# The low parts of the weights in the RWKV stage: computed by GpSimd, not by VectorE

## The chip, the cores and the metric

The kernel runs on one core of a Trainium2 chip. A core has TensorE (PE, matrix multiplication; its loading of weights is shown apart, as PEld), VectorE (DVE), ScalarE (ACT), GpSimd (POOL), the sync engine SP, whose queue issues most of the DMAs, and 16 DMA engines. Each engine works through its own instructions in order and waits on semaphores for the others. The metric is the time of one execution on the device, in microseconds, and less is better.

## The reference

It computes one step of a decoder layer with four head groups side by side, for a prompt of 1024 tokens and for 8 samples of one token each. Cut to what matters here:

```python
h = rmsnorm(x)
p = h @ w_in                       # one projection, split into columns of the four groups
out_a = diff_attn(...)             # A: differential attention
# B: RWKV-7, a recurrent state per head
s = s * w_t + (s @ a_t) * b_t + v_t * k_t
y = s @ r_t
out_b = group_norm(y) ... * silu(rg)
out_m = ssd_scan(...)              # C: Mamba-2
out_x = cross_attention(...)       # X: 256 memory tokens
x = x + concat(out_a, out_b, out_m, out_x) @ w_out
y = rmsnorm(x)
```

All of it is in float32. The results are the two outputs and the new caches and states.

## The kernel before, in words

The projection with `w_in` and the one with `w_out` are the bulk of the work on PE. To keep the accuracy of float32, each operand is split into a high part and a low part, and each product is made of three matmuls: high by high, high weight by low activation, low weight by high activation. In the profile they are `acc<-hh,whi`, `acc<-hl,whi` and `acc<-hh,wlo` (line 564). The activations are split once and stay in SBUF (`hh`, `hl`), in three groups of 344 token columns.

The weights come in pieces: 512 rows by 128 columns, held as a tile of 128 x 512. A piece is loaded by a DMA of SP's queue (`raw`, line 524), ACT makes the high part by a copy with rounding (`whi`, line 540), and DVE makes the low part, `raw` minus `whi` (`wlo`, line 541). `piece` asks for the next piece's split when it hands out the current one, so that PE has a whole piece of matmuls, 36 in the usual case, in which the next one is prepared. `raw`, `whi` and `wlo` have two buffers each.

The rest of the layer runs in stages beside the projections. A `Driver` takes turns: generators ("lanes") issue the instructions of the mixers, and between them it issues matmuls of the projection, a batch at a time. Each lane yields an estimate of how long it wants to let pass, and `K.now` counts the time of the matmuls issued. The framework then puts the instructions of each engine in order by priority and by its own estimate of when each is ready; the order on each engine is fixed before the program runs. An instruction that moves to another engine thus also moves others.

The change is in the stage of group B (RWKV), opened as `pool("bp")` in `step`. Its lanes are `elements` (for each of 16 units of 64 tokens: decays, normalised keys `kk`, the products `ar` and `bk`), `products` (Gram matrices `p_gram`, the inverse of a triangular block by doubling, the state `S` and the outputs), `norm` (the group norm of each unit's `y`) and `lane_b` (the 8 samples). The doubling in `products` is a chain between PE and DVE: PE adds to `p_t` (line 186 by the helper `mm`), DVE transposes a part of it (`xc`, line 970) and multiplies it with a mask (`lt`, line 972), ACT copies the other part (`rt`, line 978), and PE adds the next product. Four such rounds stand in each unit, after a first one whose `lt` is made in lines 950 to 952.

POOL has little to do in the stage: it fills and copies small tiles (`pe` line 885, `pc` line 888, `rt` line 954, `evx` line 706), raises to the power -1/2 in `powm` (line 216, for `rn` in `elements` and `gst` in `norm`), and issues the DMAs of the samples' states (lines 1162 and 1183). DVE waits for the powers: `rx` (line 799) for `rn`, and `y` (line 1087) for `gst`.

Of the kernel before, what the change touches and what calls it, by code (L numbers as in the profile page):

```python
# [11 lines left out]
F32 = mybir.dt.float32  # L12
# [3 lines left out]
ALU = mybir.AluOpType  # L16
# [116 lines left out]
class Kern:  # L133
# [363 lines left out]
    def plan_weights(self):  # L497

        p, w = [], self.I["w_in"]
        for name, j in ORDER[:FIRST] + ORDER:  # L500
            p += [(w, OFF[name] + j * 128, 8 if name == "mdt" else 128, kp) for kp in KO_IN]
        for i in range(2):
            for cb in range(16):
                p += [(self.I["w_out"], cb * 128, 128, kp) for kp in KO_OUT]
        self.plan, self.at, self.loaded, self.raw, self.split = p, 0, 0, {}, {}
        self.ahead, self.large, self.more = 2, None, None

    def load_pieces(self, to):
        while self.loaded < min(to, len(self.plan)):
# [17 lines left out]
    def split_piece(self, i):  # L527
        if i >= len(self.plan):
            return
        nc, m = self.nc, self.plan[i][2]  # L530
        raw = self.raw.pop(i)
        hi = self.wp.tile([128, KP, 128], F32R, name="whi", tag="whi")
        if m == 8:
            nc.vector.memset(raw[:, :, 8:32], 0.0)
            nc.scalar.copy(hi[:, :, :32], raw[:, :, :32])
            nc.vector.tensor_tensor(hi[:, :, 32:40], raw[:, :, :8], hi[:, :, :8].bitcast(F32), op=ALU.subtract)
            self.split[i] = hi, None
            return
        lo = self.wp.tile([128, KP, 128], F32R, name="wlo", tag="wlo")
        nc.scalar.copy(hi, raw)  # L540
        nc.vector.tensor_tensor(lo, raw, hi.bitcast(F32), op=ALU.subtract)  # L541
        self.split[i] = hi, lo

    def piece(self, src, c0, kp):
# [546 lines left out]
def shift_out(K, P):  # L1091

    nc = K.nc
    e = P.tile([9, 1664], F32, name="she", tag="she")
    for a in range(0, 13, 4):
        n = min(4, 13 - a)
        yield 0.5
        p = K.ps("p_sh", 1)
        for j in range(n):
            K.tp(p[:9, j * 128:j * 128 + 128], K.rawB[:, a + j, :], K.id)  # L1100
        nc.scalar.copy(e[:, a * 128:(a + n) * 128], p[:9, :n * 128])
    nc.sync.dma_start(out=K.O["shift_prompt"], in_=e[0:1, :])
    nc.sync.dma_start(out=K.O["shift_sample"], in_=e[1:9, :])
# [870 lines left out]
def projections(K):  # L1974

    W = K.I["w_in"]
    allg = list(range(NG))
    gates = {"rg": (4, "b"), "dg": (0, "a"), "xg": (12, "x")}
    evac = dict(dk=lambda j: EvPlain(K.sA[4 + j]), dv=lambda j: EvPlain(K.sA[8 + j]), dq=lambda j: EvPlain(K.sA[j], 0.125),
                mxbc=EvConv, mz=lambda j: EvSilu(K.sg[j]), xq=lambda j: EvPlain(K.sX[j], 128 ** -0.5), rs=EvShift)  # L1980

    def ready(*names):
        for n in names:
            while not K.have(n):
                yield False


    yield from ready("macc", *(f"h{g}" for g in FIRST_G))
    for name, j in ORDER[:FIRST]:
        yield from K.block(W, OFF[name] + j * 128, FIRST_G, evac[name](j), KO_IN)  # L1990
        K.turn += 1
    yield from ready("h1", "h2")
    for i, (name, j) in enumerate(ORDER):
        if name == "mdt":
            yield from K.block_dt()
        else:
            if name in gates:
                o, m = gates[name]
                yield from ready(m, "s" + m)
                ev = EvGate(o + j)  # L2000
            else:
                ev = evac[name](j)
            yield from K.block(W, OFF[name] + j * 128, [g for g in allg if i >= FIRST or g not in FIRST_G], ev, KO_IN)
        K.mark(f"{name}{j}")


def lane_x(K):

    pool = lambda n: K.tc.tile_pool(name=n, bufs=1)
    yield from K.wait("xq3", 9.00)  # L2010
    with pool("xap") as P:
        a, b = mixer_x(K, P, (0, 1)), mixer_x(K, P, (2, 3))
        for _ in range(200):
            for g in (a, b):
                r = next(g, "end")
                if r != "end":
                    yield r * 0.7
    K.mark("x")


def lane_b(K):

    pool = lambda n: K.tc.tile_pool(name=n, bufs=1, side="right")
    yield from K.wait(f"rs{RS[-1]}", 2.0)
    with pool("so") as P:
        yield from shift_out(K, P)
    yield 14.00
    with pool("sbp") as P:
        yield from samples_b(K, P)
    K.mark("sb")  # L2030


def lane_dt(K, P, P2):
    K.dt = yield from mamba_dt(K, P, P2)


def lane_m(K):
    yield from K.wait("mz3", 0.00)
    with K.tc.tile_pool(name="mmp", bufs=1, side="right") as P:
        yield from mixer_m(K, P, K.dt)  # L2040
    K.mark("m")


def lane_sa(K):

    pool = lambda n: K.tc.tile_pool(name=n, bufs=1, side="right")
    with pool("sap") as P:
        yield from samples_a(K, P)
    K.mark("sa")
    with pool("sxp") as P:  # L2050
        yield from samples_x(K, P)
    K.mark("sx")


def lane_s(K):
    yield 10.0
    with K.tc.tile_pool(name="mmr", bufs=1) as P:
        yield from samples_m(K, P, K.dt)
    K.mark("sm")


def step(ctx, tc, I, O):
    K, nc = Kern(ctx, tc, I, O), tc.nc
    pool = lambda n: tc.tile_pool(name=n, bufs=1)
    K.plan_weights()
    D = Driver(K, projections(K))
    with pool("xp") as P:
        mem = K.memory(P)
        next(mem)
        D.run([K.load_h(P), mem], batch=8)  # L2070
    with pool("ap") as P:
        D.run([mixer_a(K, P)], batch=8)
    with pool("cst") as P:
        K.cst[1] = P.tile([128, CST[1].shape[1]], F32, name="cst1", tag="cst1")
        nc.sync.dma_start(out=K.cst[1], in_=I["cst1"])
        D.run([lane_x(K), lane_sa(K)], batch=8)
    with pool("bp") as P:
        D.run(Rwkv(K, P).lanes() + [lane_b(K)], batch=4, slack=SLACK)
    with pool("mdt") as P:
        with pool("mdp") as P2:  # L2080
            D.run([lane_dt(K, P, P2)])
        D.run([lane_m(K), lane_s(K)], batch=4)
    output(K, D)
# [53 lines left out]
```

## Time and profile before

| | |
|---|---|
| time, median of 3 runs | 2157.11 us (2155.78 to 2159.48) |
| the profiled execution | 2158.15 us, its span 2156.4 us |
| PE busy in the span | 2091.5 us (97%) |
| PEld busy | 1983.5 us (92%) |
| DVE busy | 1146.5 us (53%) |
| ACT busy | 840.2 us (39%) |
| POOL busy | 201.2 us (9%) |
| mean granted TensorE clock | 0.991 of full speed |

The span runs from the first instruction to the last. PE is busy nearly all the time, so an engine beside it matters where PE stands still for it; how much that is in a stage is the difference between the stage's length and PE's busy time in it. A busy PE is not a PE at its peak, as matmuls overlap in the records: the mean of one accumulating matmul is 325 ns, while they follow each other at about half of that.

### The profile page before, as it was taken

To read this page: it belongs to the slowest core of one execution; us is meant where nothing else is said; L and a number is where in the kernel's file an instruction comes from. 1 tells how busy PE (TensorE), PEld (TensorE's weight loads), DVE (VectorE), ACT (ScalarE), POOL (GpSimd) and SP (SyncE) were. 2 spreads that over 40 slices of the span, in tenths; PEclk is the share of its full clock that TensorE was granted. 3 is DMA by queue.
4 is the path that set the end of the run, shared out by engine and by line. 5 is a ranking of instruction groups with operands and counts; after the bars stand their busy time and mean duration, and the time that the engine had idled before them with its cause. 6 is when DMAs were issued, how large, how long until landed. Compare 5 with 4: busy or idle time off the path is not lost.

```text
span 2156.4 us, 41670 instructions
## 1 busy us (share of the span) xinstructions
PE 2091.5 (97%) x16260; PEld 1983.5 (92%) x16260; DVE 1146.5 (53%) x2795; ACT 840.2 (39%) x2231; POOL 201.2 (9%) x286
## 2 busy tenths in 40 slices
PE   8999999999999999999999999998999999999997
PEld 6799999999999989988888888898999999999997
DVE  6814353543753152168977776656865254333554
ACT  7724353443233112145454454432112144333544
POOL 2100000000621320111110001001100000000000
PEclk9999999999999999999999999999999999999999
DMA  8653435242953562423322222226554763222891
GB/s 263 190 135 87 129 89 139 78 117 68 272 149 93 153 197 71 130 66 77 75 61 61 53 61 59 60 75 168 159 147 118 204 212 107 74 68 74 243 247 53
DMA packets 336925, 263.12 MB, mean 122 GB/s; under 512 B 62204, under 2 KB 310986, under 8 KB 336032
## 3 DMA queue, kind: packets, MB, share of 16 engines
q1 hardware_dynamic: 323744, 218.64, 36.2%
q0 software_dynamic: 12320, 40.28, 6.4%
q8 instruction: 128, 2.10, 0.4%
q10 hardware_dynamic: 664, 1.54, 0.2%
q14 instruction: 69, 0.57, 0.1%
HBM read 205.65 MB, written 54.80 MB: 121 GB/s over the span
## 4 chain that ended last, share of the span: by engine, by line
PE 80%; DVE 7%; DMA 3%; ACT 3%; issue 3%; POOL 1%; SPq 0%; ACTq 0%; DVEq 0%; POOLq 0%
PE acc L564 64%; PE p_s L1506 2%; PE p_t L186 2%; PE p_o L186 2%; DVE evc L715 1%; DVE wlo L541 1%; PE p_wt L190 1%; PE p_out L190 1%; PE acc L582 1%; DMA raw<-in_w_in 1%; PE p_xo L186 1%; POOL gst L216 1%; PE p_yd L186 1%; PE p_w L186 0%; PE p_xs L186 0%
## 5 line engine op out<-in xcount | busy, mean ns | idle before, releaser
L564 PE MATMUL acc<-hh,whi 128*128 128x344 f32 x3312 | 1074.7, 325 | 11.2 <-ACT haB L682 4.6
L564 PE MATMUL acc<-hl,whi 128*128 128x344 f32 x3312 | 1079.2, 326 | 0.1
L564 PE MATMUL acc<-hh,wlo 128*128 128x344 f32 x3312 | 1077.5, 325 | 0.8 <-DVE wlo L541 0.2
L564 PEld LDWEIGHTS acc<-hh,whi 128*128 128x128 f32 x3312 | 625.6, 189 | 17.3 <-ACT haB L682 4.8
L564 PEld LDWEIGHTS acc<-hl,whi 128*128 128x128 f32 x3312 | 626.9, 189 | 6.5 <-issue 1.4
L564 PEld LDWEIGHTS acc<-hh,wlo 128*128 128x128 f32 x3312 | 623.8, 188 | 7.7 <-DVE wlo L541 2.6
L541 DVE TENSOR_TENSOR wlo<-raw,whi 128x512 fp32r<-128x512 f32 x300 | 207.2, 691 | 476.5 <-ACT whi L540 468.0
L540 ACT CAST whi<-raw 128x512 fp32r<-128x512 f32 x300 | 185.5, 618 | 459.3 <-PE acc L564 392.5
L186 PEld LDWEIGHTS p_t<-rt,lt 64*64 64x64 f32 x1280 | 44.8, 135 | 33.1 <-issue 13.2
L1830 ACT ACTIVATE p_out<-xo 128x128 f32<-128x128 f32 (+1 forms) x144 | 39.8, 277 | 79.5 <-DVE xo L1829 75.1
L186 PE MATMUL p_t<-rt,lt 64*64 64x64 f32 (+1 forms) x1280 | 54.6, 224 | 15.2 <-DVE lt L972 8.4
L1509 DVE CUSTOM_DVE_ANT_0 ae<-p_s,al 128x512 f32<-128x512 f32 (+3 forms) x96 | 49.6, 554 | 34.6 <-PE p_s L1506 34.6
L1829 DVE TENSOR_TENSOR xo<-xo,p_out 128x128 f32<-128x128 f32 (+1 forms) x144 | 39.4, 280 | 26.6 <-PE p_out L190 26.4
L1516 ACT ACTIVATE ae<-ae,am 128x128 f32<-128x128 f32 (+7 forms) x64 | 49.2, 772 | 11.0 <-DVE am L1513 10.9
L978 ACT COPY rt<-p_t 128x256 f32<-128x256 f32 x64 | 22.0, 343 | 76.5 <-DVE xc L970 72.4
L216 POOL TENSOR_TENSOR osr<-osr,mhalf 128x1 f32<-128x1 f32 (+1 forms) x9 | 6.3, 721 | 472.8 <-DMA xo<-in_x_prompt 349.0
L541 DVE TENSOR_TENSOR wlo<-oraw,whi 128x512 fp32r<-128x512 f32 x48 | 33.2, 692 | 31.7 <-ACT whi L540 31.4
L216 POOL TENSOR_TENSOR ass<-ass,mhalf 128x8 f32<-128x8 f32 x4 | 6.6, 1641 | 423.3 <-DVE ass L1557 423.3
L1506 PE MATMUL p_s<-akm,aqt 128*128 128x512 f32 (+3 forms) x192 | 45.1, 359 | 0.0
L1617 POOL DMA_INDIRECT savp<-in_cache_diff_v,sapt x32 | 34.1, 1064 | 109.1 <-PE p_sao L186 100.5
L540 ACT CAST whi<-oraw 128x512 fp32r<-128x512 f32 x48 | 29.6, 617 | 32.4 <-PE acc L564 31.1
L1832 DVE TENSOR_TENSOR xo<-xo,fgc 128x128 f32<-128x128 f32 (+1 forms) x96 | 27.0, 288 | 28.7 <-ACT p_out L1830 26.2
(467 smaller groups left out, 2597.2 us busy)
## 6 DMA issues: line engine op xcount, KB each, us to landing
raw<-in_w_in SPq DMA_DIRECT2D x220, 256.0 KB
raw<-in_w_out SPq DMA_DIRECT2D x80, 256.0 KB
oraw<-in_w_out SPq DMA_DIRECT2D x12, 1024.0 KB
evm<-sm SPq DMA_DIRECT2D x48, 172.0 KB
sB<-evs SPq DMA_DIRECT2D x39, 172.0 KB
sA<-evp SPq DMA_DIRECT2D x36, 172.0 KB
evo<-so SPq DMA_DIRECT2D x36, 172.0 KB
sm<-evo SPq DMA_DIRECT2D x36, 172.0 KB
```

What stands on the lines that cost most here:

```text
L186: self.nc.tensor.matmul(out, lhsT=lhsT, rhs=rhs, start=start, stop=stop, **k)
L190: self.nc.tensor.transpose(out, in_, ident)
L216: self.nc.gpsimd.tensor_tensor(out, x, self.mhalf[:P, :n], op=ALU.pow)
L540: nc.scalar.copy(hi, raw)
L541: nc.vector.tensor_tensor(lo, raw, hi.bitcast(F32), op=ALU.subtract)
L564: nc.tensor.matmul(acc[g][:, :G], lhsT=x[:, k, :], rhs=y, start=kp == ko[0] and k == 0 and x is hi and y is a, stop=kp == ko[-1] and k == ...
L1506: nc.tensor.matmul(p[:, :k1 - k0], lhsT=qt[:, a, c], rhs=km[:, c, k0:k1], start=a == 0, stop=a == 1)
L1509: nc.vector.tensor_tensor_reduce(e[:, c, k0:k1], p[:, :k1 - k0], al[:, x0:x0 + k1 - k0], 1.0, -3e38, ALU.add, ALU.max, m[:, c, pc:pc + 1])
L1516: nc.scalar.activation(e[:, c, :nk], e[:, c, :nk], AF.Exp, bias=m[:, c, 0:1], accum_out=z[:, c:c + 1])
L1617: nc.gpsimd.indirect_dma_start(out=dst, out_offset=None, in_=I[src].rearrange("a p c -> (a p) c"), in_offset=bass.IndirectOffsetOnAxis(ap= ...
L1829: nc.vector.tensor_tensor(xt, xt, q[:n, k * 128:k * 128 + 128], op=ALU.add)
L1830: nc.scalar.activation(q[:n, k * 128:k * 128 + 128], xt, AF.Square, accum_out=self.ss[:n, 3 * g + k, cb:cb + 1])
```

## The change

A flag `low_pool` is added, which is false outside the RWKV stage. While it is set, `split_piece` gives the subtraction of line 541 to POOL in place of DVE. The operation, its operands and the two buffers stay.

```diff
--- before.py
+++ after.py
@@ -503,7 +503,7 @@
             for cb in range(16):
                 p += [(self.I["w_out"], cb * 128, 128, kp) for kp in KO_OUT]
         self.plan, self.at, self.loaded, self.raw, self.split = p, 0, 0, {}, {}
-        self.ahead, self.large, self.more = 2, None, None
+        self.ahead, self.large, self.more, self.low_pool = 2, None, None, False
 
     def load_pieces(self, to):
         while self.loaded < min(to, len(self.plan)):
@@ -538,7 +538,7 @@
             return
         lo = self.wp.tile([128, KP, 128], F32R, name="wlo", tag="wlo")
         nc.scalar.copy(hi, raw)
-        nc.vector.tensor_tensor(lo, raw, hi.bitcast(F32), op=ALU.subtract)
+        (nc.gpsimd if self.low_pool else nc.vector).tensor_tensor(lo, raw, hi.bitcast(F32), op=ALU.subtract)
         self.split[i] = hi, lo
 
     def piece(self, src, c0, kp):
@@ -2075,7 +2075,9 @@
         nc.sync.dma_start(out=K.cst[1], in_=I["cst1"])
         D.run([lane_x(K), lane_sa(K)], batch=8)
     with pool("bp") as P:
+        K.low_pool = True
         D.run(Rwkv(K, P).lanes() + [lane_b(K)], batch=4, slack=SLACK)
+        K.low_pool = False
     with pool("mdt") as P:
         with pool("mdp") as P2:
             D.run([lane_dt(K, P, P2)])
```

The instructions of every engine up to the RWKV stage and after it keep their order; within it, the order changes on all engines. 55 subtractions move. Three places follow.

On DVE, in the fourth unit; `evc` and `evx` are parts of the convolution's evacuation, `stt`, `sst` and `sy` belong to the samples. Before, a stretch with one `wlo`:

```order
L970 STREAM_TRANSPOSE xc<-p_t 128x128
L720 SCALAR_TENSOR_TENSOR evx<-evx,evc 128x344
L715 SCALAR_TENSOR_TENSOR evc<-evx,der,evc 128x344
L541 TENSOR_TENSOR wlo<-raw,whi 128x512
L972 TENSOR_TENSOR lt<-xc,cst_9329 128x256
L720 SCALAR_TENSOR_TENSOR evx<-evx,evc 128x344
L1178 TENSOR_TENSOR stt<-sst,svec 128x512
L774 TENSOR_SCALAR ld<-ld 128x512
```

The same stretch now:

```order
L970 STREAM_TRANSPOSE xc<-p_t 128x128
L720 SCALAR_TENSOR_TENSOR evx<-evx,evc 128x344
L715 SCALAR_TENSOR_TENSOR evc<-evx,der,evc 128x344
L972 TENSOR_TENSOR lt<-xc,cst_9329 128x256
L1180 TENSOR_REDUCE sy<-stt 128x8
L720 SCALAR_TENSOR_TENSOR evx<-evx,evc 128x344
L970 STREAM_TRANSPOSE xc<-p_t 128x128
L1164 TENSOR_TENSOR stt<-sst,svec 128x512
```

The `wlo` is gone from in front of `lt`, and the samples' instructions stand at other places around it.

On POOL, early in the stage, around the power `rn` of the second unit. Before:

```order
L885 MEMSET pe 128x4
L888 COPY pc<-pe 128x4
L216 TENSOR_TENSOR rn<-rn,mhalf 128x4
L954 COPY rt<-cst_9329 128x128
L706 MEMSET evx 128x3
L885 MEMSET pe 128x4
```

The same stretch now:

```order
L885 MEMSET pe 128x4
L888 COPY pc<-pe 128x4
L541 TENSOR_TENSOR wlo<-raw,whi 128x512 x3
L216 TENSOR_TENSOR rn<-rn,mhalf 128x4
L954 COPY rt<-cst_9329 128x128
L541 TENSOR_TENSOR wlo<-raw,whi 128x512
L706 MEMSET evx 128x3
L885 MEMSET pe 128x4
```

Three subtractions now stand in a row in front of `rn`, and one behind the copy `rt`.

On PE, in a later unit, where `p_t` is the doubling chain and `p_kn` the norm of the next unit's keys; the difference, with - for before and + for now:

```order
 L564 MATMUL acc_10753<-hh_1_969,wlo 128x344
 L564 MATMUL acc_10753<-hh_1_980,whi 128x344
+L186 MATMUL p_t<-rt,lt 64x2x32 x8
 L190 MATMUL p_kn<-cst_129,kk 128x128 x2
 L564 MATMUL acc_10753<-hl_1_981,whi 128x344
 L564 MATMUL acc_10753<-hh_1_980,wlo 128x344
-L186 MATMUL p_t<-rt,lt 64x2x32 x8
 L564 MATMUL acc_10753<-hh_1_988,whi 128x344
 L564 MATMUL acc_10753<-hl_1_989,whi 128x344
```

The round of `p_t` moves forward past two accumulating matmuls and `p_kn`.

## Rows read from the trace of the kernel before

**Rows 1.** Stretches of the RWKV stage: length, busy us (count) by engine, clock, DMA

```profile
908.00:1458.00 550.00, 532.76 (x6077) 476.78 (x6077) 392.77 (x1038) 251.45 (x750) 62.17 (x111) 1.00 0.26 67
...
950.00:1110.00 160.00, 151.19 (x1791) 134.93 (x1790) 138.58 (x371) 77.97 (x239) 24.61 (x45) 1.00 0.28 70
1110.00:1210.00 100.00, 95.46 (x1104) 84.99 (x1100) 73.28 (x195) 49.94 (x150) 8.83 (x18) 0.98 0.22 56
1210.00:1458.00 248.00, 244.11 (x2882) 220.38 (x2882) 162.25 (x423) 105.84 (x313) 23.37 (x38) 1.00 0.25 65
```

**Rows 2.** Waits of PE in the stage: us in total, times, longest

```profile
PE p_t L186 <- DVE lt L972: 8.4, 10, 2.3
PE p_t L186 <- DVE lt L952: 2.7, 7, 0.8
```

**Rows 3.** Time line of DVE: start, us, engine, line, operation, idle before

```profile
1009.85 0.69 DVE L541 TENSOR_TENSOR wlo<-raw,whi 128x512 fp32r<-128x512 f32 x1
...
1049.52 0.69 DVE L541 TENSOR_TENSOR wlo<-raw,whi 128x512 fp32r<-128x512 f32 x1
1050.13 0.42 DVE L972 TENSOR_TENSOR lt<-xc,cst 128x256 f32<-128x256 f32 x1
...
1397.67 0.68 DVE L541 TENSOR_TENSOR wlo<-raw,whi 128x512 fp32r<-128x512 f32 x1
```

**Rows 4.** Time line of PE at the same three places

```profile
1012.35 0.45 PE L186 MATMUL p_t<-rt,lt 64*64 64x64 f32 x8 [0.44 <-ACT evc L713]
...
1050.69 0.68 PE L186 MATMUL p_t<-rt,lt 64*64 64x64 f32 x16 [2.26 <-DVE lt L972]
...
1399.18 0.48 PE L186 MATMUL p_t<-rt,lt 64*64 64x32 f32 x10 [0.61 <-DVE lt L972]
```

**Rows 5.** Line 541 from 893 to 1458: ns min/median/max; then idle before it, times

```profile
L541 DVE TENSOR_TENSOR wlo<-raw,whi x58: 651/691/731, 894.3 to 1454.5; 128x512 fp32r<-128x512 f32 x58
...
  ACT whi L540: 41.2, 24
```

**Rows 6.** Operations of POOL by line: ns min/median/max, first and last start

```profile
L1270 POOL TENSOR_TENSOR lt<-cst,cst x1: 2381/2381/2381, 1455.9 to 1455.9; 128x1024 f32<-128x1024 f32 x1
...
L888 POOL COPY pc<-pe x16: 184/194/1496, 930.1 to 1380.5; 128x4 f32<-128x4 f32 x16
...
L216 POOL TENSOR_TENSOR gst<-gst,mhalf x17: 549/1108/1352, 982.7 to 1443.5; 128x4 f32<-128x4 f32 x16, 64x1 f32<-64x1 f32 x1
L216 POOL TENSOR_TENSOR rn<-rn,mhalf x16: 1005/1008/1392, 931.3 to 1396.4; 128x4 f32<-128x4 f32 x16
```

**Rows 7.** Time lines of POOL and of DVE around 936 us

```profile
935.46 1.50 POOL L888 COPY pc<-pe 128x4 f32<-128x4 f32 x1 [0.35 <-ACT pe L886]
...
936.16 0.41 DVE L822 TENSOR_TENSOR ksq<-ksq,pt 128x256 f32<-128x256 f32 x1
936.49 0.41 DVE L894 TENSOR_TENSOR bk<-rkv,pi 64x256 f32<-64x256 f32 x1
936.91 0.42 DVE L893 SCALAR_TENSOR_TENSOR bk<-ta,pi 64x256 f32<-64x256 f32 x1
```

**Rows 8.** Groups of DVE in the stage: count, busy us, mean ns, idle before

```profile
L972 DVE TENSOR_TENSOR lt<-xc,cst 128x256 f32<-128x256 f32 x64 | 26.9, 421 | 1.3
...
L952 DVE TENSOR_TENSOR lt<-x,cst 128x256 f32<-128x256 f32 x16 | 6.7, 419 | 0.1
```

**Rows 9.** Time lines of DVE and of PE's weight loads around 930 us

```profile
927.74 0.69 DVE L541 TENSOR_TENSOR wlo<-raw,whi 128x512 fp32r<-128x512 f32 x1 [6.03 <-ACT whi L540]
...
931.03 0.19 PEld L564 LDWEIGHTS acc<-hh,wlo 128*128 128x128 f32 x1
```

**Rows 10.** Waits of DVE for POOL in the stage

```profile
DVE rx L799 <- POOL rn L216: 15.5, 16, 1.1
DVE y L1087 <- POOL gst L216: 10.7, 14, 1.1
```

**Rows 11.** Waits of the sync engine's queue in the stage

```profile
SPq L524 <- DVE wlo L541: 143.3, 31, 11.7
```

## The prediction

> **What bounds the kernel now.** The table by stretches was read first [rows 1]. The RWKV stage, in which the change lies, runs from 908 to 1458 us. TensorE (PE) is busy for 532.76 of these 550.00 us, so it stands still for 17.24 us, and no change to another engine can win more than that here. The same table shows that VectorE (DVE) is busy for 138.58 of 160 us early on (950 to 1110, 87%), for 73% of the next 100 us and for 65% of the rest. PE's idle time follows it: 8.81, 4.54 and 3.89 us in the three stretches.
>
> The waits of PE come next [rows 2]. It waited 10 times for the tile `lt` of line 972 (8.4 us) and 7 times for that of line 952 (2.7 us). These are the right-hand steps of the block inversion in `products`: PE makes `p_t`, DVE transposes it (`xc`), DVE multiplies (`lt`), PE goes on. No wait of PE for `wlo` stands in this view of the stage.
>
> Then the time lines, to see whether a `wlo` lies in front of those steps. The longest standstill, 2.26 us at 1050.69 [rows 4], is of that kind: DVE began `wlo` at 1049.52 and the `lt` that PE wanted only at 1050.13, 0.61 us later [rows 3]. Of 27 standstills of more than 0.15 us in the stage, 12 have a `wlo` on DVE in the three microseconds before; the first is at 1012.35 (0.44 us) and the last at 1399.18 (0.61 us) [rows 3, 4].
>
> **The change, part by part.** It takes 55 subtractions off DVE (58 stand in the trace from 893 on, of 0.691 us in the median [rows 5], and the new order has 55 on GpSimd, POOL). That is 55 x 0.69 = 38 us of DVE time. DVE also stood 41.2 us, 24 times, waiting for the cast that a `wlo` needs [rows 5]; that standstill leaves its queue as well. What of this lies on the path? Only the 12 standstills of PE: each can shrink by DVE's pitch of 0.61 us or by its own length where that is shorter, 6.7 us together. The new order gives part of that back: at many places it issues the RWKV matmuls one to four accumulating matmuls earlier. I take half, **-3.3 us**. Bounds: 0, and all of the idle time, -17.2.
>
> How long is one subtraction on POOL? No such shape stands in the trace. The nearest row is the one tensor-tensor operation on 128x1024, 2.38 us alone [rows 6]; half the columns make 1.19 us. From below, DVE's own time for this shape is 0.69 [rows 5]; from above, the longest extra time that a POOL copy suffered is 1.31 us (next paragraph), so 2.5. I take 1.19, because it is the same operation with two inputs. 55 x 1.19 = 65 us, 12% of the stage.
>
> POOL and DVE do get into each other's way. The 128x4 copy `pc` takes 0.19 us in the median but took 1.50 once, at 935.46 [rows 6, 7]; at that time DVE ran `ksq` and `bk` one behind the other, each with two inputs in SBUF, the last of this run ended at 936.90, and the copy ended at 936.96 [rows 7]. So a `wlo` on POOL will wait for the end of such a run. What the trace does not show is the reverse, DVE held by a long read of POOL: the 2.38 us operation had DVE idle beside it. The hint is small, `bk` at 936.91 began 0.42 us after the one before, which itself had followed at 0.33 [rows 7]. The Trainium skill's page "SBUF — State Buffer", in its section "Who interferes with whom", speaks against the change here: a DVE instruction with two SBUF inputs and a GpSimd instruction that reads SBUF exclude each other, and the later one is blocked for the whole of the other. By that rule each of the 55 may hold DVE for 1.19 us where the old one took 0.61; without it the next term is nothing.
>
> The hold, priced from rows: `lt` has two inputs in SBUF, and PE waits for it directly. 64 of line 972 and 16 of line 952 [rows 8] make 80; POOL is inside a `wlo` for 12% of the stage, so 9.6 are met, each for half of 1.19 us on average, 5.8 us. PE waited at 17 of the 80 before [rows 2], so some have slack: I take half, **+2.9 us**. Bounds: 0, and 5.8 plus what other held instructions hand on.
>
> Next, POOL's own queue. The 33 powers `rn` and `gst` (16 and 17, 1.0 to 1.1 us [rows 6]) now share it with the `wlo`, in order. DVE waited 15.5 and 10.7 us for them already [rows 10], standing each time with all its later work behind it. 33 x 12% x half of 1.19 = 2.4 us more, of which half reaches PE: **+1.2 us** (bounds 0 and 2.4). Behind a `wlo` that itself waits for the cast it can be more; such a place is the third of three `wlo` in a row that stand in front of the second `rn`.
>
> Is the `wlo` itself late for PE? The cover is the preparation one piece ahead. The tightest of the 55 ends at 928.43 and its first weight load is at 931.03, 2.60 us later [rows 9]; a piece lasts 10 us on the average (550 us for 55). The longer duration (0.5 us) and a run of DVE in front (1.31) fit into it: 0, or about 2 us if the first pieces are met. The sync queue issues the next weight load behind `wlo` (143.3 us of waiting there [rows 11], with the loads of `rkv` behind it); half a microsecond to two later, against those 10 us, I cost it at nothing. Where that cover is gone, PE stands before the first use of a piece for what is missing.
>
> TensorE's clock was 0.98 of full speed from 1110 to 1210 [rows 1]; 2 us of lost speed more or fewer is part of the range.
>
> Sum: -3.3 + 2.9 + 1.2 = +0.8 us. The profiled execution took 2158.15 us (its span is 2156.4, the rest lies around it), so 2158.95; the median of the runs is 1.04 lower, 2157.11, so **2158 us** in runs.
>
> **The rivals.** The first, on the slower side: DVE held by POOL becomes the limit in the dense stretch. From 950 to 1110, with DVE at 87%, nearly every `wlo` meets two-input work, so each costs DVE 1.19 instead of 0.61. 15 of the 55 fall there: 15 x 0.58 = 8.7 us, all on the path because nothing is idle there to take it; of the other 40 a fifth, 40 x 0.58 x 0.2 = 4.6, and the gain is gone. +13 us, 2170. It decides once `lt` and `bk` wait about 0.6 us for each `wlo` on the average, the point at which the relief of 0.61 is used up. For it speaks the copy of 1.50 us; against it that DVE kept its turn over four instructions there, so POOL may get in mostly when DVE has a pause. By the rule of the Trainium skill's page named above, which gives the shared port to whoever starts first, this rival happens wherever POOL starts first; no run here shows how often.
>
> The second, on the faster side: DVE is hardly held, because POOL starts in DVE's pauses (13% to 35% of the time [rows 1]), and the freed 38 us and the removed standstills for the cast shorten the steps. Then the 6.7 us come in full and some of the other standstills shrink: -7 to -10, about 2149. For it speaks that most of PE's idle time lies where DVE is fullest; against it that the order was moved forward with the relief.
>
> The third: `wlo` late for PE behind a power or a DMA issue on POOL, up to 3 us at the few pieces with under 5 us of slack, 2163. Little speaks for it: nobody waited for a `wlo` in this stage. That the subtractions stay on DVE is excluded by the order.
>
> **How the numbers follow.** About 0.2% (4.3 us) is what a measurement of this kernel tells from no change. Forecast, within 0.2%: 0.46, with its own range 2153 to 2162. First rival, together with mixed cases between it and the forecast: 0.26; third rival 0.04; so slower 0.30. Second rival: 0.24, faster. The range that leaves out one in ten on either side reaches to most of both: 2149 to 2169.
>
> **What would show it.** `wlo` on POOL at 1.2 us where it is alone, 2 us and more in front of DVE's runs; if it is under 0.8, the price is wrong. Durations of `lt`, `evc` or `bk`, or pauses before them, grown by up to 1.2 us show the hold; unchanged ones speak for the second rival. DVE's waits for `rn` and `gst` should grow from 26 us to about 29. PE's idle time in the stage should stay near 17 us: at 10 the second rival holds, at 25 or more the first. PE waiting for `wlo` would show the third. If the time outside the stage moves by more than 3 us, the whole account is wrong.

## The result and the profile after

The changed kernel takes 2175.69 us (median of 6 runs, 2171.59 to 2181.75), the kernel before 2156.76 beside it (6 runs, 2152.37 to 2165.87). The ratio is 1.0081, with a 95% interval of 1.0065 to 1.0096: slower, by some 17 to 19 us, and outside the predicted range. The profiled execution took 2175.99 us, its span is 2174.2. One execution of all the runs below, of the one called early, was slow (5145.85 us) and counts in no ratio.

All of it lies in the stage. From the first use of the first moved piece by PE to the last use of the last, it takes 551.06 us (929.23 to 1480.29) where it took 529.31 (931.03 to 1460.34); the time in front of it shrank by 1.8 us and the time behind it by 2.1. The stretches of the stage in the profile after, with the columns of [rows 1]:

```profile
908.00:1480.00 572.00, 538.89 (x6078) 481.44 (x6077) 391.73 (x986) 251.89 (x749) 131.75 (x164) 0.99 0.25 65
950.00:1110.00 160.00, 144.38 (x1631) 128.58 (x1631) 130.47 (x331) 71.49 (x219) 41.91 (x58) 0.95 0.26 65
1110.00:1210.00 100.00, 93.30 (x1115) 83.09 (x1115) 74.62 (x183) 48.60 (x145) 21.67 (x27) 1.00 0.22 55
1210.00:1480.00 270.00, 260.56 (x3040) 234.94 (x3039) 167.15 (x427) 114.40 (x337) 59.07 (x67) 1.00 0.24 64
```

PE stands still for 33.11 us (572.00 less 538.89) and not for 17.24. Its granted clock in the dense stretch is 0.95 and not 1.00. Most telling is DVE: 55 subtractions are gone, 38 us of work by [rows 5], and yet its busy time over the stage is 391.73 us where it was 392.77. Something has filled the 38 us up again.

The moved operation itself, POOL's line 541 (ns min/median/max, first and last start, then POOL's idle time in front of it), and the two `lt` groups of DVE with their longest one:

```profile
L541 POOL TENSOR_TENSOR wlo<-raw,whi x55: 1263/1287/1655, 926.0 to 1468.5; 128x512 fp32r<-128x512 f32 x55
...
  ACT whi L540: 205.8, 47
```

```profile
L972 DVE TENSOR_TENSOR lt<-xc,cst x64: 389/424/1950, 948.6 to 1446.3; 128x256 f32<-128x256 f32 x64
L952 DVE TENSOR_TENSOR lt<-x,cst x16: 411/420/1517, 945.3 to 1435.7; 128x256 f32<-128x256 f32 x16
```

A subtraction takes 1.29 us. `lt` has its old median of 0.42, but single ones take 1.5 and 1.95. The time lines around the 1.95 us one, of DVE, POOL and PE in turn (start, us; in brackets the idle time in front and who ended it):

```profile
987.77 0.65 DVE L1178 TENSOR_TENSOR stt<-sst,svec 128x512 f32<-128x512 f32 x1
988.34 0.41 DVE L1069 TENSOR_TENSOR ob<-ob,bon 128x256 f32<-128x256 f32 x1
988.67 1.95 DVE L972 TENSOR_TENSOR lt<-xc,cst 128x256 f32<-128x256 f32 x1
990.54 0.68 DVE L880 TENSOR_TENSOR_SCAN ld<-cst,ld 128x256 f32<-128x256 f32 x1
...
```

```profile
989.05 1.27 POOL L541 TENSOR_TENSOR wlo<-raw,whi 128x512 fp32r<-128x512 f32 x1
```

```profile
990.76 0.45 PE L186 MATMUL p_t<-rt,lt 64*64 64x64 f32 x8 [2.60 <-DVE lt L972]
```

`lt` should have ended at 989.09. It ends at 990.62, 0.29 us behind POOL's subtraction at 990.33, and PE stands for 2.60 us. This repeats all over the stage. Counting DVE instructions that took over 0.1 us longer than the median of the same instruction before gives 39, with 32.3 us of extra time in sum, against one with 0.13 us before. Of the 35 subtractions up to 1290 us 30 overlap one (31 instructions, 28.3 us, about 1.05 us for most); of the 20 behind that, 8 do (4.0 us). Only 7 of the 39 are `lt` (5.6 us); the others are `evc`, `x`, `kk`, `bk`, `evd`, `stt`, six with one input (copies `rx` and tensor-scalar operations such as `ld`), and so on. A held instruction does its whole work behind the read: of the 19 with two inputs of 128x256, 18 end 0.28 or 0.29 us after the subtraction that they overlap, and the five of 128x344 0.37 us after it.

PE's waits for `lt`, and DVE's for the powers, in the columns of [rows 2, 10]:

```profile
PE p_t L186 <- DVE lt L972: 13.8, 11, 2.6
PE p_t L186 <- DVE lt L952: 9.0, 11, 2.8
```

```profile
DVE rx L799 <- POOL rn L216: 17.0, 15, 2.1
DVE y L1087 <- POOL gst L216: 11.7, 15, 1.5
```

The waits for `lt` doubled, from 11.1 to 22.8 us. Those for the powers went from 26.2 to 28.7. PE waited for no `wlo`: in the tightest case the subtraction starts at 925.99, takes 1.28, and its first weight load is at 929.23, 1.96 us after its end.

The clock, in stretches of the profile after (the last three numbers are the granted clock, the DMA share and GB/s):

```profile
988.00:992.40 4.40, 1.79 (x25) 1.60 (x24) 4.40 (x8) 1.69 (x5) 2.55 (x5) 1.00 0.64 141
992.40:995.80 3.40, 3.40 (x25) 2.91 (x24) 1.67 (x6) 0.03 (x1) 2.10 (x3) 0.50 0.20 49
995.80:999.20 3.40, 3.40 (x76) 3.18 (x75) 2.05 (x6) 0.30 (x2) 0.28 (x1) 1.00 0.17 43
```

After the standstill of 2.60 us that ended at 990.76, the clock goes to 0.50, the lower of its two levels (1.2 and 2.4 GHz), for 3.4 us in which PE runs 25 matmuls, and 76 in the next 3.4 us. Such a drop stands five times in the stage after (at 992.4, 1023.1, 1057.2, 1070.9 and 1091.4, each within 1.7 us of the end of a standstill of 1.6 to 2.8 us) and once before (1179.9). It does not follow every standstill: one of 2.26 us in the kernel before [rows 4] and one of 1.66 us at 1193.6 here had none behind them. Four more drops, 13.7 us at half speed, are worth about 6.8 us by the granted clock. With the 15.9 us of idle time that is 22.7, against 21.75 measured.

### The profile page after: what moved, and what is told of

Same layout as the page of the kernel before. It is cut to its first block, busy times and chain, and to the rows that moved or that the text cites. A ratio compares the mean times of both kernels' runs of the same rounds, so it can differ in the third digit from the quotient of the medians.

```text
span 2174.2 us, 41653 instructions
## 1 busy us (share of the span) xinstructions
PE 2094.9 (96%) x16260; PEld 1987.2 (91%) x16260; DVE 1144.8 (53%) x2740; ACT 840.6 (39%) x2231; POOL 270.2 (12%) x341
## 5 line engine op out<-in xcount | busy, mean ns | idle before, releaser
L541 DVE TENSOR_TENSOR wlo<-raw,whi 128x512 fp32r<-128x512 f32 x245 | 169.4, 691 | 454.1 <-ACT whi L540 439.0
L541 POOL TENSOR_TENSOR wlo<-raw,whi 128x512 fp32r<-128x512 f32 x55 | 73.3, 1332 | 205.9 <-ACT whi L540 205.8
L186 PE MATMUL p_t<-rt,lt 64*64 64x64 f32 (+1 forms) x1280 | 55.2, 226 | 26.2 <-DVE lt L972 13.8
L715 DVE SCALAR_TENSOR_TENSOR evc<-evx,der,evc 128x344 f32<-128x344 f32 (+1 forms) x72 | 43.7, 611 | 1.5 <-ACT evc L713 1.0
```

Source lines behind the costliest of these rows:

```text
L186: self.nc.tensor.matmul(out, lhsT=lhsT, rhs=rhs, start=start, stop=stop, **k)
L541: (nc.gpsimd if self.low_pool else nc.vector).tensor_tensor(lo, raw, hi.bitcast(F32), op=ALU.subtract)
L715: nc.vector.scalar_tensor_tensor(e[:, :n], x[:, t:t + n], w(t), e[:, :n], op0=ALU.mult, op1=ALU.add)
```

## The experiments

Three theories stood at the start. Theory 1: POOL's reads hold DVE's instructions (the prediction's first rival). Theory 2: the new order, in which RWKV matmuls on PE are issued earlier, costs the time. Theory 3: POOL's queue does, in which the powers now stand behind subtractions that wait for the cast. All edits are to the changed kernel; "lengthened" is counted as above, in the run's own profile. The low parts of the other stages are untouched in all of them. Where the order on an engine is compared, it is by operation, tile names and shapes in the traces.

| run | on POOL, for one piece | DVE lengthened: count, us | ratio to before (95%) |
|---|---|---|---|
| the changed kernel | subtraction, 1.29 us | 39, 32.3 | 1.0081 (1.0065 to 1.0096) |
| left out | nothing | none found | 0.9988 (0.9975 to 1.0001) |
| write only | two fills, 0.53 each | 15, 3.6 | 0.9986 (0.9973 to 0.9999) |
| write behind the cast | 4 columns copied, two fills | 6, 1.9 | 0.9966 (0.9950 to 0.9982) |
| half | subtraction 0.73, fill 0.31 | 30, 14.1 | 1.0018 (1.0004 to 1.0033) |
| copy | two copies, 0.62 each | 54, 19.6 | 1.0038 (1.0021 to 1.0056) |
| quarters | four subtractions, 0.46 each | 73, 16.7 | 1.0071 (1.0046 to 1.0096) |
| early / late / last | subtraction in a part of the stage | 25, 21.6 / 15, 10.6 / 8, 3.5 | 1.0046 / 1.0027 / 1.0015 |

**Left out.** Nobody computes the low part in the stage, and the high part stands in for it; POOL and DVE are both relieved, and the new order stays for the most part (778 of 16,260 matmuls on PE stand at another place).

```diff
-        (nc.gpsimd if self.low_pool else nc.vector).tensor_tensor(lo, raw, hi.bitcast(F32), op=ALU.subtract)
-        self.split[i] = hi, lo
+        self.low_pool or nc.vector.tensor_tensor(lo, raw, hi.bitcast(F32), op=ALU.subtract)
+        self.split[i] = hi, hi[:, :, :] if self.low_pool else lo
```

> In the RWKV stage nobody computes the low parts (the third matmul of each product reads the high part in its place, so the result is not the layer's); outside the stage all is as before. PE and DVE follow the order of the changed kernel, DVE is relieved of the 55 subtractions, and POOL reads nothing long. Theory 1 (POOL's long reads hold DVE's two-input instructions): no stretched DVE instruction, PE idle in the stage 10 to 17 us, 2150 to 2158 us. Theory 2 (the order on PE, moved forward, makes the waits): PE idle about 33 us as in the changed kernel, 2170 to 2176. Theory 3 (POOL's queue, with the powers behind the subtractions): 2150 to 2158 as by theory 1.

Measured 2156.84 us (10 runs) against 2159.58. The loss is gone. This also shows how little it gives to take 38 us off DVE: 2.6 us, with an interval that reaches no change.

**Write only.** POOL fills the low part twice instead of computing it.

```diff
-        (nc.gpsimd if self.low_pool else nc.vector).tensor_tensor(lo, raw, hi.bitcast(F32), op=ALU.subtract)
+        [nc.gpsimd.memset(lo.bitcast(F32), 0.0) for _ in range(2)] if self.low_pool else nc.vector.tensor_tensor(lo, raw, hi.bitcast(F32), op=ALU.subtract)
```

> As the changed kernel, but POOL fills each low part with zeros, twice, in place of the subtraction: it writes and does not read, about 2 x 0.53 us in the same queue positions (the product with the low part is lost). Theory 1: like the run that leaves the low parts out, 2150 to 2159 us, no stretched DVE instruction, although POOL is busy for about as long. Theory 2: 2170 to 2176. Theory 3: about 2168 to 2175, since the powers and copies stand behind POOL work of nearly the same length; DVE's waits for rn and gst as in the changed kernel (28.7 us).

Measured 2155.02 us (10 runs). The order on PE is that of the changed kernel but for 36 of 16,260 places, and POOL is at work for 58 us where it was 73, but writes only: no loss. That speaks against theory 2. Its weak point is that these fills didn't wait for the cast, so that POOL's queue was not quite the same; the run "write behind the cast" below mends that.

**Twice.** DVE computes the low part as before, and POOL the same subtraction again into a spare tile.

```diff
-        (nc.gpsimd if self.low_pool else nc.vector).tensor_tensor(lo, raw, hi.bitcast(F32), op=ALU.subtract)
+        nc.vector.tensor_tensor(lo, raw, hi.bitcast(F32), op=ALU.subtract); self.low_pool and nc.gpsimd.tensor_tensor(self.scratch, raw, hi.bitcast(F32), op=ALU.subtract)
```

> The low parts stay on DVE as before; POOL does each subtraction a second time into a tile that nobody reads. PE and DVE follow the order of the kernel before, nearly to the instruction. Theory 1: DVE keeps its 38 us and is held on top, by about 0.6 us for each of the 55: PE idle 35 us or more in the stage, 2175 to 2190 us. Theory 2: nothing changes, 2155 to 2160. Theory 3: in between, 2162 to 2175, with the powers late.

Measured 2201.8 us (4 runs) against 2159.58, ratio 1.0202 (1.0183 to 1.0220), more than the expected 2175 to 2190. The order on PE is that of the kernel before but for 131 places, so the reading on POOL costs time in the old order too. Line 541 in its profile (ns min/median/max):

```profile
L541 DVE TENSOR_TENSOR wlo<-raw,whi x300: 642/692/2225, 71.2 to 2083.2; 128x512 fp32r<-128x512 f32 x150
L541 POOL TENSOR_TENSOR scratch<-raw,whi x55: 1250/1723/2201, 928.3 to 1487.7; 128x512 f32<-128x512 f32 x55
```

Both engines wait for the same cast, start together, and each lengthens the other: DVE's 0.69 us becomes up to 2.23, POOL's 1.25 up to 2.20. The hold goes both ways.

**DVE and write.** DVE computes the low part, POOL fills a spare tile twice (`self.scratch` again); PE and DVE have exactly the order of before.

> The low parts stay on DVE as before; POOL fills a tile that nobody reads with zeros, twice, for each of the 55. PE and DVE follow exactly the order of the kernel before. Theory 1: writing alone does not hold DVE, 2154 to 2160 us, PE idle 15 to 20 us in the stage. Theory 2: the same. Theory 3: POOL's queue is as long as in the changed kernel, 2162 to 2175, with DVE's waits for rn and gst grown to over 30 us.

Measured 2161.95 us (10 runs), ratio 1.0009 (0.9994 to 1.0025). It fits theory 1 but proves little: nothing held the fills back, and all of them ran between 908.9 and 976.7 us, not beside the whole stage.

**Quarters.** The same subtraction, in four of 128x128; the order on PE and DVE is exactly that of the changed kernel.

```diff
-        (nc.gpsimd if self.low_pool else nc.vector).tensor_tensor(lo, raw, hi.bitcast(F32), op=ALU.subtract)
+        [nc.gpsimd.tensor_tensor(lo[:, k], raw[:, k], hi[:, k].bitcast(F32), op=ALU.subtract) for k in range(KP)] if self.low_pool else nc.vector.tensor_tensor(lo, raw, hi.bitcast(F32), op=ALU.subtract)
```

> GpSimd does each low part in four subtractions of 128x128 instead of one of 128x512; the order on TensorE and VectorE is that of the changed kernel. Theory 1 (VectorE's two-input instructions are held while GpSimd reads): a held instruction now waits for at most one quarter, about 0.35 us, and can go in between the quarters, though four of them can each hold somebody. If what counts is the length of one hold, the loss falls to a third or less, 2160 to 2165 us; if what counts is the total time in which GpSimd reads, which is the same or a little longer, the time stays at 2170 to 2178. Rival (GpSimd's queue is late because it stands waiting for the cast in front of the powers): nothing changes, 2175, and no VectorE instruction is shorter than in the changed kernel.

Measured 2172.73 us (7 runs) against 2156.75: nearly the whole loss is still there. One place shows why. In the changed kernel (DVE, then POOL, then PE):

```profile
1088.88 0.38 DVE L1087 TENSOR_TENSOR y<-y,gst 128x256 f32<-128x256 f32 x1
1089.19 0.42 DVE L951 TENSOR_TENSOR x<-x,cst 128x256 f32<-128x256 f32 x1
1089.52 1.48 DVE L785 TENSOR_TENSOR kk<-rkv,pt 128x256 f32<-128x256 f32 x1
1090.92 0.41 DVE L952 TENSOR_TENSOR lt<-x,cst 128x256 f32<-128x256 f32 x1
```

```profile
1089.31 1.41 POOL L541 TENSOR_TENSOR wlo<-raw,whi 128x512 fp32r<-128x512 f32 x1 [2.07 <-ACT whi L540]
```

```profile
1091.48 0.37 PE L186 MATMUL p_t<-rt,lt 64*64 64x64 f32 x2 [2.79 <-DVE lt L952]
```

The same place with quarters:

```profile
1093.02 0.57 DVE L1087 TENSOR_TENSOR y<-y,gst 128x256 f32<-128x256 f32 x1
1093.51 0.67 DVE L951 TENSOR_TENSOR x<-x,cst 128x256 f32<-128x256 f32 x1
1094.11 0.67 DVE L785 TENSOR_TENSOR kk<-rkv,pt 128x256 f32<-128x256 f32 x1
1094.70 0.67 DVE L952 TENSOR_TENSOR lt<-x,cst 128x256 f32<-128x256 f32 x1
```

```profile
1092.85 2.23 POOL L541 TENSOR_TENSOR wlo<-raw,whi 128x128 fp32r<-128x128 f32 x4 [1.99 <-ACT whi L540]
```

```profile
1095.52 0.37 PE L186 MATMUL p_t<-rt,lt 64*64 64x64 f32 x2 [3.28 <-DVE lt L952]
```

In the changed kernel one instruction is held for 1.06 us, and it isn't `lt` but `kk` in front of it. With quarters the two engines take turns, and each of four DVE instructions pays 0.15 to 0.25 us, 0.9 in sum. In a queue of two-input instructions it is the sum of the holds that arrives at `lt`, so cutting them up saves little. Compared instruction by instruction on PE, from the stage's start, with the run "write behind the cast", the changed kernel is 13 us late by about 1095 us and 20 by 1290, and the quarters 17 and 18: where DVE is fullest they cost more (four take 1.85 us alone, in place of 1.29), and behind that they lose only 1 us more in place of 7. So the time fell into the range that was expected if the total of the reading counts; that the length of one hold decides where DVE has pauses is read from this one profile.

**Late and early.** POOL computes the low parts only from the ninth unit on (27 in the profile), or only in the first eight (28).

```diff
-            K.mark(f"b_e{it}")
+            K.mark(f"b_e{it}"); K.low_pool = it >= 8
...
-        K.low_pool = True
+        K.low_pool = False
```

(For the first eight it is `it < 8`, and the flag stays true at the start.)

> Low parts on GpSimd from the ninth unit of 64 tokens on, 22 subtractions of the 55; before that they stay on VectorE. In this part VectorE is about 65% busy. Theory 1: few two-input instructions stand ready when GpSimd reads, so the loss is small, 0 to 5 us over the kernel before, 2156 to 2162, with under 10 us of stretched VectorE instructions. Rival (every subtraction on GpSimd costs the same, 19 us / 55 = 0.34 us each, wherever it stands): +7.5, 2165.

> Low parts on GpSimd in the first eight units alone, about 33 subtractions of the 55, where VectorE is 73 to 87% busy. Theory 1 with the dense stretch as the place of the loss: 12 to 19 us over the kernel before, 2168 to 2176. Rival (the same cost for each): 33 x 0.34 = +11, 2168. The losses of this and of the late one should add up to that of the changed kernel, about 19 us, whichever holds.

Measured 2163.53 us (10 runs; ratio 1.0027, 1.0007 to 1.0047) and 2168.12 (9 runs; 1.0046, 1.0029 to 1.0063). The two excesses make 1.0073 together, close to the 1.0081 of the whole: the loss adds up over the pieces. The late one lost a little more than theory 1 foresaw, the early one less than its 12 to 19 us. By the medians that is 0.41 us for each early subtraction and 0.25 for each late one. The two times alone don't decide between the theory and an equal price for each.

**Last.** Only from the twelfth unit on (18 subtractions, from 1295 us), `it >= 11`. PE's order is that of before.

> Low parts on GpSimd from the twelfth unit on, 18 subtractions, with TensorE's order that of the kernel before. Against the run whose fills only write, the changed kernel lost 13 us up to 1110, 10 from there to 1290 and 0.3 behind it. Theory 1 with that reading (a hold costs only where VectorE has a queue that TensorE waits for): 2154 to 2159, no loss. Rival (each subtraction on GpSimd costs about 0.3 us wherever it stands): +5 to 6, 2162.

Measured 2163.36 us (10 runs) against 2160.44, ratio 1.0015 (0.9999 to 1.0031): inconclusive, for the interval holds both nothing and the rival's 5 to 6 us (0.23 to 0.28%). Its profile has 8 lengthened instructions (3.5 us), and PE is 1.15 us later at the end of the stage than before, matched instruction by instruction. In that one profile theory 1 is the nearer, but it is of the fastest of the ten executions, and the part is no gain either way.

**Copy.** POOL copies the raw piece to the low part twice, with one input instead of two; the product with the low part is lost.

```diff
-        (nc.gpsimd if self.low_pool else nc.vector).tensor_tensor(lo, raw, hi.bitcast(F32), op=ALU.subtract)
+        [nc.gpsimd.tensor_copy(out=lo, in_=raw) for _ in range(2)] if self.low_pool else nc.vector.tensor_tensor(lo, raw, hi.bitcast(F32), op=ALU.subtract)
```

> In place of the subtraction GpSimd copies the raw piece to the low part twice, so it reads one input of 128x512 in SBUF twice where it read two at once; the low part of the product is then not what it should be. Order nearly that of the changed kernel. Theory 1 in its wide form (any long read of GpSimd from SBUF holds VectorE's two-input instructions): loss as in the changed kernel, 2166 to 2178, with 20 us or more of stretched VectorE instructions. In its narrow form (it takes two inputs on GpSimd): as with the two fills that only write, 2154 to 2159, and the two-input instructions unstretched.

Measured 2164.73 us (10 runs) against 2156.75: between the two forms that were expected, so neither size was met. The kind is clear from the profile, though. 54 instructions are lengthened by 19.6 us, `evc` and `lt` with their two inputs among them, and the fills of the other runs did nothing of the sort: one input read by POOL is enough to hold them. A single copy lasts 0.62 us, so a hold is shorter, and the copies don't wait for the cast.

**Write behind the cast.** POOL copies four columns of the high part, for which it waits as the subtraction does, and then fills twice.

```diff
+        [nc.gpsimd.tensor_copy(out=lo[:, 0, 0:4], in_=hi[:, 0, 0:4].bitcast(F32))] + [nc.gpsimd.memset(lo.bitcast(F32), 0.0) for _ in range(2)] if self.low_pool else nc.vector.tensor_tensor(...)
```

> The low part in the RWKV stage is zero: GpSimd copies 4 columns of the high part, so that it waits for the cast as the subtraction does, and then fills the low part twice (0.53 us each in the earlier run), so it is busy for about as long as with the subtraction and stands in front of the powers in the same way, but reads next to nothing. Theory 1 (the reads of GpSimd hold VectorE): as with the fills that did not wait, 2153 to 2159 us, PE waiting 10 to 12 us for lt. Theory 3 (GpSimd's queue: the powers behind a low part that waits for the cast): the loss comes back, 2170 or more, with VectorE's waits for rn and gst grown from 28 us to well over 30.

Measured 2156.10 us (10 runs) against 2160.44. Line 541 on POOL, PE's and DVE's waits in its profile:

```profile
L541 POOL MEMSET wlo<- x110: 516/526/687, 930.5 to 1452.1; 128x512 f32 x110
L541 POOL CAST wlo<-whi x55: 183/188/702, 930.3 to 1451.2; 128x4 fp32r<-128x4 f32 x55
...
  ACT whi L540: 193.3, 45
```

```profile
PE p_t L186 <- DVE lt L972: 7.9, 8, 2.1
...
PE p_t L186 <- DVE lt L952: 2.1, 8, 0.3
```

```profile
DVE rx L799 <- POOL rn L216: 17.3, 15, 2.2
...
DVE y L1087 <- POOL gst L216: 11.7, 16, 1.1
```

POOL waits for the cast as long as in the changed kernel (193.3 and 205.8 us), works as long on each piece, and DVE waits just as long for the powers (29.0 and 28.7 us). Yet PE's waits for `lt` are 10.0 us and not 22.8, and nothing is lost. Theory 3 falls, and theory 2 with it: PE's order is that of the changed kernel but for 50 of 16,260 places. (On DVE, with the low parts left out, 202 of 2,447 places differ. The profile is of the slowest of the ten executions, 2161.92 us.) At the place shown above, DVE in this run:

```profile
1081.84 0.42 DVE L785 TENSOR_TENSOR kk<-rkv,pt 128x256 f32<-128x256 f32 x1
1082.17 0.42 DVE L951 TENSOR_TENSOR x<-x,cst 128x256 f32<-128x256 f32 x1
1083.18 0.42 DVE L1087 TENSOR_TENSOR y<-y,gst 128x256 f32<-128x256 f32 x1 [0.59 <-POOL gst L216]
1083.53 0.42 DVE L952 TENSOR_TENSOR lt<-x,cst 128x256 f32<-128x256 f32 x1
```

All four have their 0.42 us. The wait for `gst` stands in front of `lt` here too (the order of the four differs a little), but PE's standstill in front of this `p_t` is only 0.40 us.

**Half.** POOL subtracts half of each piece and fills the other half.

```diff
+        [nc.gpsimd.tensor_tensor(lo[:, 0:2], raw[:, 0:2], hi[:, 0:2].bitcast(F32), op=ALU.subtract), nc.gpsimd.memset(lo[:, 2:4].bitcast(F32), 0.0)] if self.low_pool else nc.vector.tensor_tensor(...)
```

> GpSimd subtracts half of each low part (128x256, about 0.7 us of reading in place of 1.29) and fills the other half with zeros (about 0.3 us of writing). Theory 1: a hold lasts half as long and the loss is near half of the changed kernel's, 8 to 12 us over the kernel before, 2164 to 2169. If only holds above some length reach TensorE because shorter ones fit into slack: 2158 to 2163. Theory 3 (the queue): 2172 or more.

Measured 2164.89 us (10 runs) against 2160.44. In sum DVE's instructions are longer by 14.1 us, where the whole subtraction made it 32.3. The ratio says 4 us of loss, under the 8 to 12 that were expected. That expectation halved the net loss of 19 us, though the relief stays whole however little POOL reads: matched instruction by instruction with "write behind the cast", PE is 7.1 us late at the end of the stage, and the changed kernel 21.6. So a third of the loss in these profiles (by the ratios 45%, 0.52 of 1.15 points) comes with 57% of the reading (0.73 of 1.29 us) and 44% of the lengthening. Less reading, less loss, and theory 3's 2172 is excluded once more.

The profile of the changed kernel holds a control of its own, which needs no second kernel. `tq` is a multiplication with a mask like `lt`, 128x256 too, but one of its inputs lies in PSUM, the memory that PE writes its results to. It began inside a subtraction and took its usual time (DVE, then POOL):

```profile
1300.96 0.39 DVE L994 TENSOR_TENSOR tq<-p_t,cst 128x256 f32<-128x256 f32 x1
```

```profile
1300.31 1.27 POOL L541 TENSOR_TENSOR wlo<-raw,whi 128x512 fp32r<-128x512 f32 x1 [1.50 <-ACT whi L540]
```

That holds throughout: of the DVE instructions that began inside a subtraction, 34 had an input in PSUM, and none took over 0.02 us more than its median; 33 had both inputs in SBUF, and 29 of them were lengthened (the other four began in its last 0.2 us). In "write behind the cast" 66 with both inputs in SBUF began inside POOL's copies and fills, and none was lengthened.

Theory 1 stands: with POOL's waits and its busy time kept, and PE's order nearly so, the loss comes with what POOL reads and goes without it. The stage alone, in the profiles, says the same: 529.3 us before, 551.1 in the changed kernel, 548.1 with quarters, 538.6 with copies, 536.6 with half, and 526.8 to 529.5 with nothing or with fills. What PE does between the hold and its standstill is read from the traces alone. No version tried here wins much by this move: with the low parts left out the ratio is 0.9988, and with POOL only writing 0.9966 at best.

## Why the prediction was wrong

**What failed is the hold.** The step priced it from `lt` alone: 80 instructions, 12% of the time, half of 1.19 us, 5.8 us, of which half, +2.9. For `lt` that came out in sum, by luck in its parts: 7 were lengthened, by 5.6 us. But `lt` stands at the end of a queue in which three instructions in five (414 of 692 from 929 to 1290 us) read two inputs from SBUF, and any of them that is held makes `lt` late, as `kk` at 1089.52. Counted over the whole queue it is 32.3 us, of which about half reached PE: idle time in the stage grew by 15.9 us, and it is 17.5 us above that of "write behind the cast". So the holds cost PE 16 to 17.5 us where the step had +2.9. The factor for slack was about right; the number of exposed instructions was not. The share of 12% was the wrong way to count as well. DVE was busy for 279.05 of the 361 us from 929 to 1290, so a subtraction did not meet `lt` by chance but met whatever DVE had next (30 of 35), and held it for about 1.05 us, not for half of its own length.

**The rival that came true is the first**, which has this mechanism and priced it at +13, 4 to 6 us under the measured loss. (The second, DVE hardly held, falls with the 39 lengthened instructions.) Its condition, about 0.6 us of waiting for each subtraction, was met (32.3 us for 55 is 0.59), and DVE's unchanged busy time says the same. I held it less likely because DVE kept its turn over four instructions around 936 us [rows 7]. That row shows POOL starting second. Nor does DVE's run end where the prediction lets it end: the next two-input `bk` starts at 936.91, so POOL's copy got in between two of them. In the changed kernel POOL's record begins before that of the held instruction in 35 of 38 cases, and then DVE waits to the end of the read.

The Trainium skill's page "SBUF — State Buffer", section "Who interferes with whom", states this lock: two SBUF inputs of DVE against a read of GpSimd, for the whole instruction, and not against a write. The traces here agree on all three: `lt` held for 1.53 us beside a subtraction of 1.27, the fills holding but one two-input instruction (by 0.27 us), and DVE and POOL each held by the other in the run "twice".

**The clock** was 2 us of the range; it was about 6.8 us, in four more drops that followed the longer standstills. This size is less sure than the rest: the run "write behind the cast" has 13.7 us at half speed in its stage without the holds, the one with fills alone 6.8, and no run changed the clock alone. But the clock is not the main cause: with 13.7 us at half speed against 17.1 that stage is 21.6 us shorter than the changed kernel's.

**The relief**, -3.3: the runs without a subtraction on either engine give ratios of 0.9966 to 0.9988, so 2.6 to 7 us (2.7 to 4.6 by the medians). The size fits; that it comes from the 12 standstills is not shown.

**The powers behind `wlo`**, +1.2: their waits went to 28.7 us, as foreseen (29). They cost nothing that can be seen, since "write behind the cast" has the same waits and no loss.

**The duration**, 1.19 us for one subtraction: 1.29. **`wlo` late for PE**, nothing: right, and PE's waits show no such line. The sync queue waits longer behind `wlo` than in [rows 11],

```profile
SPq L524 <- POOL wlo L541: 198.4, 41, 13.9
```

and no more came of it than the step said, since "write behind the cast" waits there too (174.3 us, for the cast) without a loss. **Outside the stage**, no more than 3 us: it is 1.8 us less in front and 2.1 less behind, 3.9 in sum, a little over the bound. The bound was too tight to tell anything: over all the profiles the part in front takes 929 to 935 us and the part behind 688 to 698.

## What to carry to other kernels

Moving work off a well filled DVE to GpSimd freed nothing here, because GpSimd reads SBUF for it: 38 us of planned DVE work, worth 2.6 to 7 us on the path, came back as 32 us of holds at places that the order written at build time did not allow for. Before such a move, ask of every DVE instruction in the queue, and not only of the last one in front of PE, whether it would be held (here those with two inputs in SBUF, and some with one, but none with an input in PSUM), and take one hold of nearly the whole read for each subtraction where DVE has few pauses. Cutting the read into four won back little (0.71% of loss in place of 0.81%).

## What was not expected of the hardware

The prediction counted instructions with two inputs. Some of DVE with one input were held as well: the copy `rx` took 1.36 and 1.38 us in the changed kernel, 0.29 usually, and the tensor-scalar operation `ld` of 128x512 up to 0.97 us more than usual. With POOL only writing, such copies and tensor-scalar instructions are nearly all that is lengthened (0.1 to 0.4 us each); of the two-input instructions a single one is, `ksq`, by 0.27 us.

Who waits depends on more than whose record begins first, and no run settled it. The `lt` shown at 988.67 began 0.38 us before the subtraction and was held all the same. At 1093 us the quarters of 0.46 us and four DVE instructions took turns. At 934.68, in the same run, one quarter took 3.04 us behind a row of DVE instructions that kept their 0.41 us. That is the behaviour of [rows 7], on which the prediction leaned.
